# Seven products of quarters for eight in one pair of chunks of a feed-forward layer's first product

## The chip, the cores and the metric

The kernel runs on one core of one Trainium2 chip. The metric is the device time of one execution in microseconds (us). The kernel before was timed in three runs: median 1037.13 us, lowest 1036.57, highest 1037.86.

## The reference, cut to what matters

The reference is a decoder trunk of two layers over 256 tokens of width 1024. Each layer is a half-step feed-forward part, a token mixing and a second half-step feed-forward part, each followed by a layer norm. Only the feed-forward part matters here; it runs four times, and each run is called a stage below.

```python
def swiglu(x, w_in, w_out):
    gate, up = jnp.split(x @ w_in, 2, axis=-1)
    return (jax.nn.silu(gate) * up) @ w_out

x = layer_norm(alpha * x + 0.5 * swiglu(x, ffn_w_in[l, 0], ffn_w_out[l, 0]), ...)
```

Here x is 256 x 1024, w_in 1024 x 5632 and w_out 2816 x 1024, all float32.

## The kernel before

**Arithmetic.** Each float32 operand is split into a high part and a low rest (`split`, L70-81): ScalarE copies the tile to the high part (L78, `wh` or `exh`), VectorE subtracts that from the tile (L79, `wl` or `exl`). A product is then three matmuls on TensorE (`mm3`: L105 high times high, L106 high times low weight, L107 low times high weight). Weights come as tiles of 128x1024 (512 KB), which SyncE's queue loads in the order of its program (`stage`, L82-87) into five buffers `wst`. The split parts live in six buffers `wh`/`wl`, or, for some tiles (`more=True`), in four further buffers `exh`/`exl`.

**First product.** The hidden width is cut into eleven chunks of 256; a chunk is 256 columns of the gate and 256 of the up half, 512 in all. The tokens are two tiles of 128. A chunk takes four weight tiles and 48 matmuls of 128x512: two token tiles, eight steps of 128 along the width 1024, three matmuls each. Chunks 0 and 1 run together, then 2 to 10 one after the other. When a chunk is summed in its PSUM bank, `act` (L248-253) makes silu(gate) on ScalarE (L250) and multiplies by the up half on VectorE (L252). Half-way through the next chunk `emit_T` transposes the result (four matmuls, L270) and splits it (`parts`, L258 on ScalarE, L259 on VectorE); for the chunks in `FAST` it also makes the sums of its quarters that the second product needs (L280-283).

**Second product.** For the chunks in `FAST` (0, 2, 4, 6, 7) `fast(c)` uses seven products of quarters where the plain form has eight: the 256 x 1024 block of weights and the activations are each seen as 2 x 2 quarters, sums of quarters are multiplied, and the seven results are combined at the end (`shared_sums`). The sums of weight quarters go into tiles of their own, `ts` (L353, L354, L357, L358). The other chunks use the plain form (`down`). The last three chunks run as a tail, token tile by token tile, and a layer norm follows.

**What sets the order.** The program is written in the order of the mathematics. A list scheduler orders each engine's instructions before the run; on the chip each engine works through its list in order, and an instruction waits there for its inputs and for the release of the buffer that it writes. PSUM has eight banks: four of `mm`, one each of `pt` and `ov`, two of `sc`.

## Time and profile before

| quantity | value |
|---|---|
| median of three runs | 1037.13 us (1036.57 to 1037.86) |
| the profiled execution: its own time | 1037.3 us |
| its span, first to last instruction | 1035.3 us |
| mean granted TensorE clock in it | 0.997 of full speed |
| TensorE matmul busy | 1018.1 us, 98% |
| VectorE busy | 784.8 us, 76% |
| ScalarE busy | 551.0 us, 53% |
| data read | 188.26 MB, 183 GB/s over the span |

An engine is busy while one of its instructions executes. Matmuls overlap one another, so a busy TensorE is not one at its peak: the distance between the starts of two matmuls tells the rate. Idle time in front of an instruction is shown in square brackets with the instruction that ended it. A stretch of the timeline is named by its time from the start of the span. The fourth stage's first product lies at 843 to 968 us, its second at 968 to 1030.

### The profile page before, as it was taken

The page shows a single profiled execution, that of the slowest core. Times are in us where ns is not written, and L with a number is a line of the kernel's source. Part 1 is how long each engine was busy: PE and PEld are TensorE (multiplying, and loading weights), DVE is VectorE, ACT ScalarE, POOL GpSimd, SP SyncE. Part 2 cuts the span into 40 slices and gives each one's busy share as a digit, 9 for nine tenths or more (in the row PEclk, how much of TensorE's full clock was granted, in tenths as well). Part 3 has the DMA queues.
Part 4 walks back from the last instruction along what each step waited for, and adds up shares of the span by engine and source line. Part 5 has one row for each costly group of instructions (what it writes and reads, how often), then busy time and mean ns, then how long its engine had stood idle before and what let it go on. Part 6 is the DMA issues. An engine that isn't in the chain of part 4 may idle for free.

```text
span 1035.3 us, 14159 instructions
## 1 busy us (share of the span) xinstructions
PE 1018.1 (98%) x5166; PEld 830.0 (80%) x5166; DVE 784.8 (76%) x1313; ACT 551.0 (53%) x916; POOL 23.3 (2%) x35
## 2 busy tenths in 40 slices
PE   9999999999999999999999999999999999999997
PEld 6888878878877888888878888888888778888785
DVE  6765978975989566687986668898679885657877
ACT  7554546435785445553644456544358744446451
POOL 0000000100000000000000000002000000000000
PEclk9999999999999999999999999999999999999998
DMA  9866646753463466674585656559515544666641
GB/s 341 295 204 185 214 148 191 263 189 114 133 230 85 165 189 182 174 232 143 171 283 163 184 183 207 178 156 326 185 34 176 187 136 152 185 190 189 197 150 41
DMA packets 59541, 190.22 MB, mean 184 GB/s; under 512 B 7120, under 2 KB 8784, under 8 KB 58704
## 3 DMA queue, kind: packets, MB, share of 16 engines
q1 hardware_dynamic: 59184, 189.07, 57.8%
q8 instruction: 40, 0.66, 0.3%
q10 hardware_dynamic: 288, 0.26, 0.1%
q14 instruction: 29, 0.24, 0.1%
HBM read 188.26 MB, written 1.05 MB: 183 GB/s over the span
## 4 chain that ended last, share of the span: by engine, by line
PE 73%; DVE 13%; DMA 7%; ACT 4%; issue 2%; DVEq 0%; ACTq 0%; SPq 0%
PE ph L107 12%; PE ph L106 12%; PE ph L105 12%; DMA wst<-in_ffout 5%; DVE wl L79 4%; PE acc L105 4%; PE acc L107 4%; PE acc L106 4%; DVE exl L79 2%; PE pj L107 2%; PE pj L105 2%; PE pj L106 2%; ACT wh L78 2%; PE ov L581 2%; PE pt L569 2%
## 5 line engine op out<-in xcount | busy, mean ns | idle before, releaser
L79 DVE TENSOR_TENSOR wl<-wst,wh 128x1024 fp32r<-128x1024 f32 (+3 forms) x276 | 304.6, 1107 | 147.5 <-ACT wh L78 144.9
L78 ACT ACTIVATE wh<-wst 128x1024 fp32r<-128x1024 f32 (+3 forms) x276 | 264.9, 968 | 233.8 <-PE ph L107 110.8
L105 PE MATMUL ph<-wh,xh 128*128 128x512 f32 x640 | 252.8, 395 | 0.3 <-ACT xh L239 0.3
L107 PE MATMUL ph<-wh,xl 128*128 128x512 f32 x640 | 250.2, 391 | 0.0
L106 PE MATMUL ph<-wl,xh 128*128 128x512 f32 x640 | 250.0, 391 | 0.0
L105 PEld LDWEIGHTS ph<-wh,xh 128*128 128x128 f32 x640 | 120.2, 188 | 25.1 <-ACT wh L154 0.7
L107 PEld LDWEIGHTS ph<-wh,xl 128*128 128x128 f32 x640 | 120.1, 188 | 25.2
L106 PEld LDWEIGHTS ph<-wl,xh 128*128 128x128 f32 x640 | 120.3, 188 | 24.5 <-DVE wl L155 0.3
L78 ACT ACTIVATE exh<-wst 128x512 fp32r<-128x512 f32 (+1 forms) x76 | 63.1, 858 | 65.9 <-PE p L107 54.3
L79 DVE TENSOR_TENSOR exl<-wst,exh 128x512 fp32r<-128x512 f32 (+1 forms) x76 | 72.1, 969 | 28.2 <-ACT exh L78 27.5
L105 PE MATMUL pj<-wh,xh 128*128 128x384 f32 (+3 forms) x224 | 78.2, 349 | 0.3
L107 PE MATMUL pj<-wh,xl 128*128 128x384 f32 (+3 forms) x224 | 77.9, 348 | 0.0
L106 PE MATMUL pj<-wl,xh 128*128 128x384 f32 (+3 forms) x224 | 77.1, 344 | 0.0
L250 ACT ACTIVATE sg<-ph 128x256 f32<-128x256 f32 x88 | 33.5, 384 | 67.1 <-PE ph L107 63.5
L252 DVE TENSOR_TENSOR g<-sg,ph 128x256 f32<-128x256 f32 x88 | 35.3, 416 | 30.0 <-ACT sg L250 29.1
L79 DVE TENSOR_TENSOR exl<-ts,exh 128x1024 fp32r<-128x1024 f32 x40 | 47.5, 1221 | 1.8 <-ACT exh L78 0.5
L105 PEld LDWEIGHTS pj<-wh,xh 128*128 128x128 f32 x224 | 42.3, 189 | 3.1 <-ACT nqS L824 0.7
L106 PEld LDWEIGHTS pj<-wl,xh 128*128 128x128 f32 x224 | 42.4, 189 | 1.8
L107 PEld LDWEIGHTS pj<-wh,xl 128*128 128x128 f32 x224 | 42.3, 189 | 1.8
L78 ACT ACTIVATE exh<-ts 128x1024 fp32r<-128x1024 f32 x40 | 40.7, 1055 | 5.8 <-PE acc L107 3.8
L218 POOL TENSOR_TENSOR mv<-mv,mhalf 128x1 f32<-128x1 f32 x12 | 11.2, 931 | 900.6 <-DVE mv L217 900.6
L548 DVE TENSOR_REDUCE nm<-sc 128x2 f32<-128x512 f32 (+2 forms) x36 | 23.0, 642 | 10.7 <-PE sc L544 10.4
(367 smaller groups left out, 1659.6 us busy)
## 6 DMA issues: line engine op xcount, KB each, us to landing
wst<-in_ffin SPq DMA_DIRECT2D x156, 512.0 KB, 4.4
wst<-in_ffout SPq DMA_DIRECT2D x88, 512.0 KB, 4.0
wst<-in_ffin SPq DMA_DIRECT2D x40, 256.0 KB, 4.0
exh<-in_w SPq DMA_DIRECT2D x16, 512.0 KB, 6.4
wst<-in_w_out SPq DMA_DIRECT2D x16, 512.0 KB, 4.7
gb<-in_lngb SPq DMA_DIRECT2D x6, 1024.0 KB, 7.2
wst<-in_w_b SPq DMA_DIRECT2D x16, 256.0 KB, 4.4
wst<-in_w_nq SPq DMA_DIRECT2D x8, 384.0 KB, 4.4
```

Source lines behind the costliest of these rows:

```text
L78: nc.scalar.activation(h[:, c], src[:, c], AF.Copy)
L79: nc.vector.tensor_tensor(out=l[:, c], in0=src[:, c], in1=h[:, c].bitcast(F32), op=OP.subtract)
L105: nc.tensor.matmul(out, lhsT=xh, rhs=wh, start=start, stop=False)
L106: nc.tensor.matmul(out, lhsT=xh, rhs=wl, start=False, stop=False)
L107: nc.tensor.matmul(out, lhsT=xl, rhs=wh, start=False, stop=stop)
L218: nc.gpsimd.tensor_tensor(out=mv[:, 3:4], in0=mv[:, 2:3], in1=mhalf[:, 0:1], op=OP.pow)
L250: nc.scalar.activation(sg, ps[:, :256], AF.Silu)
L252: nc.vector.tensor_tensor(out=g, in0=sg, in1=ps[:, 256:], op=OP.mult)
L548: nc.vector.tensor_reduce(out=nm[:, :n], in_=sv, axis=AX.X, op=OP.max, negate=True)
L569: nc.tensor.transpose(pt[:, b * P:(b + 1) * P], pr[:, b * P:(b + 1) * P], ident)
L581: order(nc.tensor.matmul(out[g * 64:(g + 1) * 64], lhsT=v, rhs=p_, start=i == 0, stop=i == n - 1, skip_group_check=True))
```

## The change

In each stage chunks 4 and 5 are computed together by `fast_pair`. The weights of the two chunks and the tokens are seen as 2 x 2 quarters: rows of the weights in halves of 512, columns by chunk, tokens by tile. Seven products of quarters replace eight, 84 matmuls of 128x512 for 96. They run in two halves `j`, each over 256 of the 512 rows of a quarter. For each half four weight tiles are loaded (`b00`, `b10`, `b01`, `b11`), four sums of 128x1024 are made in place in those buffers, and seven tiles of 128x1024 are split where four would be. Seven PSUM banks hold the products. At the end ScalarE copies one (`u1`) and VectorE makes seven sums of 128x512 from the banks.

The sums of token quarters are made once a stage after chunks 0 and 1 (`pair_operands`): on VectorE four instructions of 128x1024 and four of 128x512, two of the former being splits, and on ScalarE two copies; they use two of the `wst` buffers for a time, and the split high part has the buffer of the layer norm's gain and bias (`gb`).

`fast(c)` of the second product makes its sums in place in the weight tiles and no longer uses `ts`. Constants and tokens of the first stage are loaded ahead of chunk 3 and not ahead of chunk 4. `g` has four buffers for three, `a10` and `su` one for two.

```diff
+PAIRS = (4,)
...
+            def pair_operands():
...
+                for t in range(2):
+                    r.append(wpool.tile([P, 1024], F32, tag="wst", name="wst", bufs=5))
+                    tt(out=r[t], in0=xTh[t].bitcast(F32).rearrange("p k s -> p (k s)"),
+                       in1=xTl[t].bitcast(F32).rearrange("p k s -> p (k s)"), op=OP.add)
+                tt(out=r[1][:, hi], in0=r[1][:, lo], in1=r[1][:, hi], op=OP.add)
+                tt(out=r[1][:, lo], in0=r[0][:, lo], in1=r[1][:, lo], op=OP.subtract)
+                tt(out=r[0][:, lo], in0=r[1][:, hi], in1=r[0][:, lo], op=OP.subtract)
+                tt(out=r[0][:, hi], in0=r[0][:, hi], in1=r[0][:, lo], op=OP.subtract)
+
+                sh = xpool.tile([P, 2, D], F32R, tag="gb", name="sh")
+                sl = fp.tile([P, 2, D], F32R, tag="sl", name="sl")
+                for t in range(2):
+                    nc.scalar.activation(sh[:, t], r[t], AF.Copy)
+                    nc.vector.tensor_tensor(out=sl[:, t], in0=r[t], in1=sh[:, t].bitcast(F32), op=OP.subtract)
...
+            def fast_pair(c, x, between):
+
+                pr = {}
+                for n in ("p1", "p7", "p2", "p4"):
+                    pr[n] = mm.tile([P, 512], F32, tag="mm", name=n)
+                for n, tag in (("p5", "pt"), ("p6", "ov"), ("p3", "sc")):
+                    pr[n] = at.tile([P, 512], F32, tag=tag, name=n, bufs=2 if tag == "sc" else 1)
+                tt = nc.vector.tensor_tensor
+                for j in range(2):
+                    b00, b10, b01, b11 = (
+                        stage(a["ffin"][l, i, c + h][:, (4 * r + 2 * j) * 512:(4 * r + 2 * j + 2) * 512], 1024)
+                        for h in range(2) for r in range(2))
...
+                    take("p1", b00, True)
+                    tt(out=b00, in0=b01, in1=b00, op=OP.subtract)
+                    tt(out=b01, in0=b11, in1=b01, op=OP.subtract)
+                    take("p5", b00, False)
+                    take("p7", b01, True)
+                    take("p3", b11, False)
+                    tt(out=b11, in0=b11, in1=b00, op=OP.subtract)
+                    take("p6", b11, True)
+                    take("p2", b10, False)
+                    tt(out=b10, in0=b10, in1=b11, op=OP.subtract)
+                    take("p4", b10, True)
+                    for n, y in (("p1", "a00"), ("p5", "s1"), ("p7", "s3"), ("p3", "s4"), ("p6", "s2"), ("p2", "a01"),
+                                 ("p4", "a11")):
+                        for k in range(2):
+                            cols = slice(k * 512, (k + 1) * 512)
+                            mm3(pr[n], (x[y][0][:, 2 * j + k], x[y][1][:, 2 * j + k]), (w[n][0][:, cols], w[n][1][:, cols]),
+                                j == 0 and k == 0, j == 1 and k == 1)
+                    if j == 0:
+                        between()
+                u1, u2, u3, u4 = (fp.tile([P, 512], F32, tag=f"u{n}", name=f"u{n}") for n in range(1, 5))
+                nc.scalar.activation(u1, pr["p1"], AF.Copy)
+                tt(out=u2, in0=u1, in1=pr["p6"], op=OP.add)
...
+                if first and cs[0] == 3:
+                    load_consts()
+                    init_consts()
+                if cs[0] in PAIRS:
+                    pend = fast_pair(cs[0], x_pair, emit_pend)
+                    continue
...
-                if first and cs == (4,):
-                    load_consts()
-                    init_consts()
...
+                if len(cs) == 2:
+                    x_pair = pair_operands()
...
             def fast(c):
...
-                tt(out=u[:, lo], in0=b0[:, hi], in1=b0[:, lo], op=OP.subtract)
-                tt(out=u[:, hi], in0=b1[:, hi], in1=b0[:, hi], op=OP.subtract)
+                tt(out=b0[:, lo], in0=b0[:, hi], in1=b0[:, lo], op=OP.subtract)
+                tt(out=b0[:, hi], in0=b1[:, hi], in1=b0[:, hi], op=OP.subtract)
                 w1 = split(b1, 1024, 1024, True)
-                wu = split(u, 1024, 1024, True)
-                tt(out=v[:, lo], in0=b1[:, hi], in1=u[:, lo], op=OP.subtract)
-                tt(out=v[:, hi], in0=b1[:, lo], in1=v[:, lo], op=OP.subtract)
-                wv = split(v, 1024, 1024, True)
+                wu = split(b0, 1024, 1024, True)
+                tt(out=b1[:, hi], in0=b1[:, hi], in1=b0[:, lo], op=OP.subtract)
+                tt(out=b1[:, lo], in0=b1[:, lo], in1=b1[:, hi], op=OP.subtract)
+                wv = split(b1, 1024, 1024, True)
```

**Where instructions stand.** On VectorE, in the fourth stage, before: the splits of chunk 4's last tile and of chunk 5 (`wl_8673` to `wl_8685` are tiles of chunk 4, `wl_8769` to `wl_8787` those of chunk 5), with the sums and the split of a transposed chunk among them.

```order
L79 TENSOR_TENSOR wl_8685<-wst_8682,wh_8684 128x1024
L259 TENSOR_TENSOR g3l_8629<-ptg_8623,g3h_8628 128x512
L79 TENSOR_TENSOR wl_8769<-wst_8766,wh_8768 128x1024
L252 TENSOR_TENSOR g_8658<-sg_8656,ph_8597 128x256
L252 TENSOR_TENSOR g_8662<-sg_8660,ph_8601 128x256
L79 TENSOR_TENSOR wl_8775<-wst_8772,wh_8774 128x1024
L79 TENSOR_TENSOR wl_8781<-wst_8778,wh_8780 128x1024
L79 TENSOR_TENSOR wl_8787<-wst_8784,wh_8786 128x1024
```

The same place of the changed kernel, the second half of the pair: the four buffers are `wst_8802` (b00), `wst_8804` (b10), `wst_8806` (b01) and `wst_8808` (b11); L81 is the split, L337 to L345 are the sums in place, `wl_8915` and `wl_8921` are the first two tiles of chunk 6.

```order
L337 TENSOR_TENSOR wst_8802<-wst_8806,wst_8802 128x1024
L338 TENSOR_TENSOR wst_8806<-wst_8808,wst_8806 128x1024
L81 TENSOR_TENSOR wl_8817<-wst_8802,wh_8816 128x1024
L81 TENSOR_TENSOR wl_8825<-wst_8808,wh_8824 128x1024
L81 TENSOR_TENSOR exl_8821<-wst_8806,exh_8820 128x1024
L342 TENSOR_TENSOR wst_8808<-wst_8808,wst_8802 128x1024
L261 TENSOR_TENSOR g3l_8799<-ptg_8793,g3h_8798 128x512
L81 TENSOR_TENSOR wl_8834<-wst_8804,wh_8833 128x1024
L81 TENSOR_TENSOR exl_8830<-wst_8808,exh_8829 128x1024
L345 TENSOR_TENSOR wst_8804<-wst_8804,wst_8808 128x1024
L81 TENSOR_TENSOR wl_8915<-wst_8912,wh_8914 128x1024
L81 TENSOR_TENSOR wl_8921<-wst_8918,wh_8920 128x1024
```

Behind these rows stands `exl_8839`, the split for the last product p4 of the pair, so two tiles of chunk 6 and four sums are now ahead of it.

On ScalarE, in the same stage, before: `wh_8485` and `wh_8491` are the high parts of chunk 3's third and fourth tile, `wh_8575` that of chunk 4's first; g0h, s0h and g1h are the parts of chunks 0 and 1.

```order
L78 ACTIVATE wh_8485<-wst_8483 128x1024
L258 ACTIVATE g0h_8364<-ptg_8352 128x384
L258 ACTIVATE s0h_8368<-su_8359 128x512
L78 ACTIVATE wh_8491<-wst_8489 128x1024
L258 ACTIVATE g1h_8435<-ptg_8430 128x512
L78 ACTIVATE wh_8575<-wst_8573 128x1024
```

The same place of the changed kernel: `exh_8719` is the high part of b00 in the first half of the pair, `wh_8616` and `wh_8622` are those of chunk 3's third and fourth tile.

```order
L80 ACTIVATE exh_8719<-wst_8711 128x1024
L260 ACTIVATE g0h_8481<-ptg_8469 128x384
L260 ACTIVATE s0h_8485<-su_8476 128x512
L80 ACTIVATE wh_8616<-wst_8614 128x1024
L80 ACTIVATE wh_8622<-wst_8620 128x1024
L260 ACTIVATE g1h_8566<-ptg_8561 128x512
```

The copy for b00 has moved ahead, and chunk 3's third tile, which was ahead of g0h and s0h, now stands behind both and that copy.

On VectorE in the second product of the fourth stage, before: one chunk of `fast`, its weight tiles being `wst_9511` and `wst_9513`.

```order
L353 TENSOR_TENSOR ts_9515<-wst_9511 128x512
L354 TENSOR_TENSOR ts_9515<-wst_9513,wst_9511 128x512
L357 TENSOR_TENSOR ts_9516<-wst_9513,ts_9515 128x512
L358 TENSOR_TENSOR ts_9516<-wst_9513,ts_9516 128x512
L79 TENSOR_TENSOR wl_9608<-wst_9605,wh_9607 128x1024
L79 TENSOR_TENSOR exl_9518<-wst_9511,exh_9517 128x512
L79 TENSOR_TENSOR exl_9524<-wst_9513,exh_9523 128x1024
```

The same chunk in the changed kernel, with the tiles `wst_9671` and `wst_9673`:

```order
L81 TENSOR_TENSOR exl_9676<-wst_9671,exh_9675 128x512
L438 TENSOR_TENSOR wst_9671<-wst_9671 128x512
L439 TENSOR_TENSOR wst_9671<-wst_9673,wst_9671 128x512
L81 TENSOR_TENSOR exl_9682<-wst_9673,exh_9681 128x1024
L81 TENSOR_TENSOR wl_9764<-wst_9761,wh_9763 128x1024
L81 TENSOR_TENSOR exl_9686<-wst_9671,exh_9685 128x1024
L442 TENSOR_TENSOR wst_9673<-wst_9673,wst_9671 128x512
L443 TENSOR_TENSOR wst_9673<-wst_9673 128x512
L81 TENSOR_TENSOR exl_9692<-wst_9673,exh_9691 128x1024
```

The four sums stood together ahead of the splits; now each stands behind the split that must have read its tile, and both weight buffers stay taken until the last two splits have read them.

## Rows read from the trace of the kernel before

**Rows 1.** The page's first section: busy time, share of the span, instructions.
```profile
PE 1018.1 (98%) x5166; PEld 830.0 (80%) x5166; DVE 784.8 (76%) x1313; ACT 551.0 (53%) x916; POOL 23.3 (2%) x35
```
**Rows 2.** What TensorE waited for: us in total, times, longest.
```profile
PE acc L105 <- DVE g10l L259: 1.8, 3, 1.1
```
**Rows 3.** Timeline of TensorE, fourth stage: start, us, instruction, idle before.
```profile
866.31 0.60 PE L270 MATMUL ptg<-ident,g 128*128 128x128 f32 x4
866.66 0.48 PE L105 MATMUL ph<-wh,xh 128*128 128x512 f32 x1
...
889.31 0.39 PE L107 MATMUL ph<-wh,xl 128*128 128x512 f32 x1
889.54 0.39 PE L105 MATMUL ph<-wh,xh 128*128 128x512 f32 x1
...
912.28 0.39 PE L105 MATMUL ph<-wh,xh 128*128 128x512 f32 x1
...
978.23 0.50 PE L105 MATMUL acc<-wh,g1h 128*128 128x512 f32 x1 [0.44 <-DVE g10l L259]
```
**Rows 4.** Groups by line and shape: busy, mean ns, idle before and releasers.
```profile
L79 DVE TENSOR_TENSOR wl<-wst,wh 128x1024 fp32r<-128x1024 f32 x204 | 249.3, 1223 | 131.8 <-ACT wh L78 129.3
L78 ACT ACTIVATE wh<-wst 128x1024 fp32r<-128x1024 f32 x204 | 215.7, 1060 | 187.4 <-PE ph L107 110.8 <-issue 29.1 <-DMA wst<-in_ffout 28.7
L353 DVE TENSOR_TENSOR ts<-wst 128x512 f32<-128x512 f32 x20 | 13.7, 683 | 0.0
```
**Rows 5.** Timeline of VectorE back to back, fourth stage.
```profile
951.13 0.68 DVE L354 TENSOR_TENSOR ts<-wst 128x512 f32<-128x512 f32 x1
951.73 1.22 DVE L79 TENSOR_TENSOR wl<-wst,wh 128x1024 fp32r<-128x1024 f32 x1
952.87 1.22 DVE L79 TENSOR_TENSOR exl<-wst,exh 128x1024 fp32r<-128x1024 f32 x1
```
**Rows 6.** Timeline of VectorE early in the second, third and fourth stage.
```profile
349.57 0.75 DVE L252 TENSOR_TENSOR g<-sg,ph 128x256 f32<-128x256 f32 x2 [7.77 <-ACT sg L250]
...
532.80 1.23 DVE L79 TENSOR_TENSOR wl<-wst,wh 128x1024 fp32r<-128x1024 f32 x1 [2.61 <-ACT wh L78]
...
861.47 0.75 DVE L252 TENSOR_TENSOR g<-sg,ph 128x256 f32<-128x256 f32 x2 [7.74 <-ACT sg L250]
...
864.92 2.54 DVE L79 TENSOR_TENSOR wl<-wst,wh 128x1024 fp32r<-128x1024 f32 x2
```
**Rows 7.** Busy time by stretch: PE, PEld, DVE, ACT, POOL; clock, DMA share, GB/s.
```profile
863.00:883.00 20.00, 20.00 (x94) 16.53 (x93) 14.31 (x19) 11.49 (x16) 0.00 (x0) 1.00 0.61 192
883.00:903.00 20.00, 20.00 (x94) 16.53 (x93) 12.38 (x19) 10.29 (x15) 0.00 (x0) 1.00 0.65 188
```
**Rows 8.** Timeline of ScalarE ahead of the pair, fourth stage.
```profile
869.71 1.06 ACT L78 ACTIVATE wh<-wst 128x1024 fp32r<-128x1024 f32 x1 [1.70 <-PE ph L107]
870.68 0.47 ACT L258 ACTIVATE g0h<-ptg 128x384 fp32r<-128x384 f32 x1
871.05 0.62 ACT L258 ACTIVATE s0h<-su 128x512 fp32r<-128x512 f32 x1
...
875.69 1.06 ACT L78 ACTIVATE wh<-wst 128x1024 fp32r<-128x1024 f32 x1 [1.71 <-issue]
```
**Rows 9.** The page's DMA issues: KB each, median us to landing.
```profile
wst<-in_ffin SPq DMA_DIRECT2D x156, 512.0 KB, 4.4
```
**Rows 10.** DMA in the stretch 5 to 30 us: packets, MB, mean rate.
```profile
DMA packets 3778, 8.98 MB, mean 359 GB/s; under 512 B 422, under 2 KB 550, under 8 KB 3776
```
**Rows 11.** Chain of work around the fourth stage's second product: start, us, what.
```profile
958.72 4.17 DMA wst<-in_ffout
...
967.73 4.09 DMA wst<-in_ffout
971.85 1.07 ACT wh L78
...
977.57 0.61 DVE g10l L259
```

48 lines of the change are left out of this document (34 added, 14 removed).

## The prediction

> **What bounds the kernel now.** I read the page's busy times first. TensorE is busy 98% of the span and VectorE 76% [rows 1]; a share is no limit yet, so I went on to TensorE's waits. Over all four stages it waits for VectorE in the second product 1.8 us in three waits, and that is its largest entry [rows 2]: TensorE practically never stops. What a matmul costs is read from starts, not from its 0.39 us of duration: 889.31 to 889.54 is one step, and the 96 matmuls and two sets of transposes of two chunks take 912.28 - 889.54 = 22.74 us [rows 3]. With 0.45 us for a set (from 866.31 to 866.66 is 0.35, and the matmul behind it runs 0.09 longer) that is (22.74 - 0.9) / 96 = 0.2275 us a matmul. So an edit that takes matmuls away is worth 0.2275 us each as long as the splits keep ahead.
>
> VectorE is the next engine. In the first product it is busy 14.3 and 12.4 us out of 20 [rows 7], and the split lies well ahead of its use: the high part of chunk 4's first tile is made at 875.69 [rows 8], its first matmul starts at 889.54 [rows 3], 13.85 us later. This lead is what the change draws on. In the second product the chain of waits runs through loads of `wst` (4.17 and 4.09 us), the splits behind them and g10l [rows 11], for which TensorE then waits 0.44 us at 978.23 [rows 3]: there the lead is already nil.
>
> **The change part by part.** *Matmuls.* 12 fewer a stage: 12 x 0.2275 = 2.73 us, 10.9 us in four stages, all on the path as long as TensorE is never made to wait.
>
> *What it adds on VectorE, in the pair.* Six more splits (14 for 8) and eight sums of 128x1024. Back to back a 128x1024 instruction starts 1.14 us behind the one before (951.73, 952.87), a 128x512 one 0.60 (951.13 to 951.73) [rows 5]; 14 x 1.14 = 16.0 us. Then seven sums of 512 from PSUM, 4.2 us by the same step (the nearest row; one that has PSUM as input may cost more). The pair's own demand is 22 x 1.14 = 25.1 us for 84 x 0.2275 + 0.45 = 19.6 us of matmuls; before it was 8 x 1.14 = 9.1 for 22.7. It goes into deficit and lives on the lead. ScalarE gains six copies (1.06 us [rows 4]) and one for u1; it had some 9 us in 20 free [rows 7].
>
> *Which lead is left.* Fourth stage, from the order and the steps above. In the changed list the copy for b00 stands ahead of g0h and s0h, and chunk 3's third tile behind them. b00's load is issued about 866.2, when the first of the splits at 864.92 [rows 6] sets a buffer free, lands 4.4 us later [rows 9] at 870.6, and only then go its copy (1.0 us), g0h and s0h (0.4 and 0.6) and that tile's copy, which started at 869.71 before, ahead of g0h at 870.68 [rows 8]; its split ends at about 875.0. It releases the buffer for b11, the fourth tile of the pair's first half, which lands at 875.0 + 4.4 = 879.4. L338 needs b11, so VectorE stands some 1.4 us before that. From 879.4 it is busy without a pause: nine 1024-instructions left of the first half, thirteen up to and with the split of p4 in the second (two tiles of chunk 6 among them), 22 x 1.14 = 25.1; the transposed chunks' sums and parts and four products by the gate 3.9; waits for copies that ScalarE has just made, 1.3 to 2.3 (each 0.3 to 0.5 us, few). That ends at 909.7 to 910.7.
>
> TensorE comes to p4 of the second half at 889.54 + 42 x 0.2275 + 0.45 + 36 x 0.2275 = 907.7, and needs the low part one matmul later. It stands 1.7 to 2.7 us; I take 2.3, as ScalarE's copy for p4 stands behind that of chunk 6's third tile, whose buffer (b00's) comes free only at about 901.2 and is loaded at 905.6. The first half is not in danger: its p4 split ends near 892.4 and is wanted at 897.7. Behind the pair the u sums and chunk 6's remaining splits cost at most 0.2 us, and by chunk 8 the lead is back, with 7 us of VectorE free in 20.
>
> *Operands of the pair.* 4 x 1.14 + 4 x 0.60 = 7.0 us on VectorE after chunks 0 and 1 start. It fits into an idle stretch of 7.74 us in the fourth stage [rows 6], and of 7.77 in the second [rows 6]. The third shows 2.61 there [rows 6]; 3 to 4 us of splits are pushed back and most of it is made up before chunk 4. I charge 0.2 us: a stall of 2.5 in the third stage, bounds 1.7 to 4.
>
> *First stage.* The constants and tokens (560 and 512 KB) now stand ahead of chunk 2's tiles in SyncE's queue, where DMA already moves 359 GB/s [rows 10]: 1.07 MB / 359 = 3.0 us during which no weights come. Chunk 2 had a lead that just bears this; the pair's b11 is then about 0.7 us later and VectorE starts with less. Stall 3.5 us, bounds 2.7 to 4.5.
>
> *Sums in place in `fast`.* The number of VectorE instructions is the same, but both weight buffers stay taken until the last two splits: for the first about 6 us longer, for the second 1 to 2. In the fourth stage the loads on the chain start when a buffer comes free (958.72, 967.73 [rows 11]), so part of that reaches g10l, which TensorE awaits: 0.4 to 0.75 us a stage, I take 0.5, 2.0 in all. It can be nil if g10l's delay comes from the splits alone, and 1 us if each load of the chain moves.
>
> *At nothing.* `a10`, `su` with one buffer: they are used once in two chunks. The layer norm's gain and bias are loaded when the pair is over, 60 us ahead of their use.
>
> *The sum,* against the profiled execution's 1037.3 us: 1037.3 - 10.9 + (2.3 + 2.3 + 2.5 + 3.5) + 2.0 = 1039.0. The median lies 0.17 us below that execution: 1038.8. With the terms' own ends the forecast runs from 1035.6 to 1042.1.
>
> *A rule beside the step of 1.14 us.* An instruction lasts 1.22 us on VectorE, but the next starts 1.14 behind it [rows 4, 5]. The Trainium skill, "VectorE: DVE Perf Modes", in its section on the DRAIN, says that the next instruction does not start until the pipe has emptied; its errata section gives (N + 151) / 0.96 ns for such an fp32 instruction, 1.224 us for 1024 by my estimate, which is this trace's duration [rows 4] and not its step. By the page's sum 22 instructions would cost 26.9 us, the stall would be 1.8 us longer in each stage and the total 1046, which is rival B. The measured step decides.
>
> **The rivals.** *A, VectorE keeps ahead.* For it: in the first product it is idle a third of the time [rows 7], and 13.85 us of lead stand against a deficit of 25.1 + 3.9 - 19.6 = 9.4; were b11 to land 2 us earlier, nothing would be late. Against it: the lead ends with the load of b11, by the order above. If stalls shrink to between nothing and 1.2 us a stage, the time is 1026.4 (1037.3 - 10.9) to about 1034; middle 1030.
>
> *B, the pair is late (slower).* The split of p4 comes 4 to 5 us after its time. Place: the second half, from b11's landing on; price 4.5 x 4 = 18 us, so 1037.3 - 10.9 + 18 + 2 = 1046.4. It decides once loads take over 6 us instead of 4.4 or the effective step is 1.22: a stall above 2.73 us a stage makes the pair a loss by itself. For it: four of five weight buffers are held by one half. Against: 0.65 of DMA is used in these stretches [rows 7] and 4.4 us is the median landing [rows 9].
>
> *C, buffers of the second product (slower).* Each of the held buffers delays the next load and TensorE stands 1 to 2 us more than now in each stage: 2 to 6 us above the forecast, 1041 to 1045. It decides if the loads at 958 and 967 [rows 11] shift by the full time that the first buffer is held longer.
>
> *D, seven products do not save.* The matmuls of the pair could start further apart, since their token operands come from other tiles; at 0.26 us (0.2275 x 96 / 84) the gain is nil and so are the stalls: 1037.3 + 2.0 = 1039. Against it: 5166 weight loads take 830.0 us [rows 1], 0.16 each, under a step of 0.2275.
>
> **How the numbers follow.** Within 0.2% (2.1 us, about what a measurement of this kernel can tell from no change) means 1035.1 to 1039.2. Forecast 0.44, of it 0.25 within and 0.19 above; A 0.33, all below 1035.1; B 0.10 and C 0.08, above; D 0.05, within. That is faster 0.33, same 0.30, slower 0.37. The range leaves out the lower half of A's span and the upper part of B: 1029 to 1046. The likeliest case's own range is 1035.6 to 1042.1.
>
> **What would show it.** Matmuls in the profile after: 48 fewer. Each step: a wait of TensorE for `exl` (the split for p4 or p6) of 2 to 3 us once in a stage, at the end of the pair; VectorE busy nearly all of the 28 us before it, and idle for a DMA landing (b11) just ahead of that stretch; chunk 6 beginning about 0.4 us earlier than now relative to chunk 4 (22.3 us for 22.74); g10l's wait in the second product at about 1 us for 0.44. If no wait for `exl` is there, A holds; if it is 4 us or more, B; if the waits grow behind 968 us, C; if the step within the pair is above 0.23, D. Wrong altogether would be a scheduler's list that the chip meets in another rhythm: b11 landing by 877, or a stall on a PSUM bank that the pair holds.

## The result and the profile after

The changed kernel takes 1065.43 us (median of 4 runs, 1062.98 to 1071.13) and the kernel before 1037.02 (median of four, one run more than above): a ratio of 1.0281, with a 95% interval of 1.0235 to 1.0326. It is slower by some 28 us. The prediction was 1038.8 with a range of 1029 to 1046, so both the time and the range were wrong. The profiled execution is the one of 1062.98 us, with a span of 1060.9 and a mean granted clock of 0.992 (before: 1035.3 and 0.997).

The page's busy line, which answers [rows 1]:

```profile
PE 1019.8 (96%) x5118; PEld 823.4 (78%) x5118; DVE 888.8 (84%) x1429; ACT 581.8 (55%) x952; POOL 22.3 (2%) x35
```

There are 48 matmuls fewer (5118 for 5166), as the diff says, yet TensorE is busy 1.7 us longer. With less to do it ran part of the time at the lower clock. What it waited for (us in total, times, longest), against [rows 2]:

```profile
PE acc L107 <- DVE g10l L261: 9.2, 4, 3.2
PE pt L240 <- DVE x L229: 9.2, 3, 6.8
PE p L107 <- ACT exh L80: 2.5, 4, 1.0
PE p L108 <- DVE exl L81: 2.4, 6, 0.5
```

L261 is the line that was L259, L229 was L227, and `p` are the banks of the pair's products. g10l, 1.8 us before, is now 9.2. The second row is new in size: the layer norm's output `x`, 6.8 us in one piece (the kernel before waits 0.8 us for it in all). The waits in the pair, around which the prediction was built, come third and fourth.

The same in TensorE's timeline (start, us, instruction, idle before), [rows 3] being its counterpart. The rows of the first block lie in the third stage's second product, the one of the second at the layer norm that ends the first stage:

```profile
669.69 0.51 PE L107 MATMUL acc<-wh,g1h 128*128 128x512 f32 x1 [3.23 <-DVE g10l L261]
...
672.10 0.63 PE L109 MATMUL acc<-wh,g1l 128*128 128x512 f32 x1
672.53 0.63 PE L107 MATMUL acc<-wh,g1h 128*128 128x512 f32 x1
...
```

```profile
201.53 1.97 PE L240 MATMUL pt<-ident,x 128*128 128x128 f32 x8 [6.78 <-DVE x L229]
```

From 672.10 to 672.53 is one step: 0.43 us, where the same step is 0.2275 at the full clock. This wait is paid twice, first as idle time and then at half rate.

To tell the stages' parts apart I use two stretches. "First" runs from TensorE's first transposition of chunk 0's result to that of chunk 10's (107.66 us in each stage before). "Rest" runs from there to the next stage's first transposition, the last one to the end of the span (219.12, 78.21, 218.37 and 61.32 us before); it holds the second product, the layer norm and the attention. Differences to before in us, profiled execution against profiled execution (the medians differ from these by a few us), for the kernels that carry the argument:

| kernel | first, stages 1 to 4 | sum | rest, stages 1 to 4 | sum |
|---|---|---|---|---|
| after | +2.3 −0.7 +1.0 +1.3 | +3.8 | +10.0 +2.8 +7.2 +1.3 | +21.3 |
| `e1_inplace`: sums in place, no pair | 0 0 0 0 | 0 | +8.9 +4.8 +5.7 +5.6 | +24.9 |
| `e2_pair`: pair, sums as before | +2.3 −1.6 −0.9 −2.3 | −2.4 | −1.7 +0.3 +3.8 −0.6 | +1.8 |
| `e9_pair_nosums`: `e2_pair` without its eight sums | −0.8 −2.6 −2.6 −2.6 | −8.6 | −1.7 +0.4 −0.2 −0.1 | −1.7 |
| `e16_three_pairs`: best version | 0 −1.6 +1.2 −2.3 | −2.7 | −1.0 −0.4 −0.2 −0.3 | −2.0 |

The loss of the changed kernel lies almost wholly in "rest", a part of the stage in which not one matmul was removed.

### The profile page after: what moved, and what is told of

Its sections match the earlier page's. It is cut to its first block, busy times and chain, and to the rows that moved or that the text cites. A ratio compares the mean times of both kernels' runs of the same rounds, so it can differ in the third digit from the quotient of the medians.

```text
span 1060.9 us, 14190 instructions
## 1 busy us (share of the span) xinstructions
PE 1019.8 (96%) x5118; PEld 823.4 (78%) x5118; DVE 888.8 (84%) x1429; ACT 581.8 (55%) x952; POOL 22.3 (2%) x35
## 3 DMA queue, kind: packets, MB, share of 16 engines
q1 hardware_dynamic: 59184, 189.07, 54.3%
## 4 chain that ended last, share of the span: by engine, by line
PE 54%; DVE 20%; DMA 13%; issue 7%; ACT 6%; POOL 0%; DVEq 0%; ACTq 0%; SPq 0%; POOLq 0%
DMA wst<-in_ffin 6%; DMA wst<-in_ffout 5%; PE ph L109 5%; PE ph L108 5%; DVE wl L81 5%; PE ph L107 5%; DVE exl L81 4%; PE acc L107 4%; PE acc L109 4%; PE acc L108 4%; PE pj L109 3%; PE pj L107 3%; PE pj L108 3%; ACT wh L80 3%; PE ov L666 2%
## 5 line engine op out<-in xcount | busy, mean ns | idle before, releaser
L81 DVE TENSOR_TENSOR wl<-wst,wh 128x1024 fp32r<-128x1024 f32 (+3 forms) x268 | 290.6, 1100 | 64.4 <-ACT wh L80 63.2
L80 ACT ACTIVATE exh<-wst 128x1024 fp32r<-128x1024 f32 (+1 forms) x148 | 137.5, 954 | 121.3 <-DVE wst L443 36.4
L107 PE MATMUL ph<-wh,xh 128*128 128x512 f32 x512 | 202.1, 397 | 1.9 <-ACT wh L80 1.6
L108 PE MATMUL ph<-wl,xh 128*128 128x512 f32 x512 | 201.1, 393 | 0.6 <-DVE wl L81 0.3
L109 PE MATMUL ph<-wh,xl 128*128 128x512 f32 x512 | 200.9, 392 | 0.0
L81 DVE TENSOR_TENSOR exl<-wst,exh 128x1024 fp32r<-128x1024 f32 (+1 forms) x148 | 158.5, 1089 | 37.4 <-ACT exh L80 36.8
L107 PEld LDWEIGHTS ph<-wh,xh 128*128 128x128 f32 x512 | 96.4, 189 | 22.4 <-ACT wh L80 1.9
L108 PEld LDWEIGHTS ph<-wl,xh 128*128 128x128 f32 x512 | 96.5, 189 | 20.9 <-DVE wl L157 0.8
L109 PEld LDWEIGHTS ph<-wh,xl 128*128 128x128 f32 x512 | 96.4, 188 | 20.1 <-DVE xl L242 0.2
L633 DVE TENSOR_REDUCE nm<-sc 128x2 f32<-128x512 f32 (+2 forms) x36 | 22.9, 642 | 10.4 <-PE sc L629 10.1
L272 PE MATMUL ptg<-ident,g 128*128 128x128 f32 x176 | 27.0, 274 | 1.3 <-DVE g L254 1.3
L272 PEld LDWEIGHTS ptg<-ident,g 128*128 128x128 f32 x176 | 21.8, 141 | 8.2 <-DVE g L254 2.2
```

The costliest lines, as they stand in the source:

```text
L80: nc.scalar.activation(h[:, c], src[:, c], AF.Copy)
L81: nc.vector.tensor_tensor(out=l[:, c], in0=src[:, c], in1=h[:, c].bitcast(F32), op=OP.subtract)
L107: nc.tensor.matmul(out, lhsT=xh, rhs=wh, start=start, stop=False)
L108: nc.tensor.matmul(out, lhsT=xh, rhs=wl, start=False, stop=False)
L109: nc.tensor.matmul(out, lhsT=xl, rhs=wh, start=False, stop=stop)
L272: nc.tensor.transpose(pt[:, at_[k][t]], gs[t][:, k * P:(k + 1) * P], ident)
```

## The experiments

Names in the diffs are those of the kernel after. In the quoted expectations a letter stands for a theory; what each holds is told around them. Each ratio is to the kernel before on the same chip.

**Which part of the change costs the time.** Three theories stood against each other: the sums in place in `fast`, VectorE's deficit in the pair, and the earlier loads of the constants. The first run leaves the pair out and keeps the sums in place. The second keeps the pair and makes the sums in `ts` again, for which `sl` has to share these two buffers. The third loads the constants ahead of chunk 4 as before.

```diff
 e1_inplace (against after)
-PAIRS = (4,)
+PAIRS = ()
...
 e2_pair (against after)
-                sl = fp.tile([P, 2, D], F32R, tag="sl", name="sl")
+                sl = [fp.tile([P, D], F32R, tag="ts", name="sl", bufs=2) for _ in range(2)]
...
-                tt(out=b0[:, lo], in0=b0[:, hi], in1=b0[:, lo], op=OP.subtract)
+                tt(out=u[:, lo], in0=b0[:, hi], in1=b0[:, lo], op=OP.subtract)
 e3_consts4 (against after)
-                if first and cs[0] == 3:
+                if first and cs[0] == 4:
```

> The changed kernel without the pair and its operands; the sums in place of the second product stay, as do the loading of the constants ahead of chunk 3 and the buffer counts. Theory S (the sums in place cost the time: a sum must wait until the split has read the tile it overwrites, and the weight buffers and the memset on GpSimd that waits for a split buffer push the layer norm's hand-over back): the kernel is slower than before by 18 to 25 us, 1055 to 1062, and shows the long wait of TensorE for the layer norm at the end of the first stage and the waits for g10l. Theory V (VectorE's deficit in the pair is never made up and carries into the second product): without the pair the time is that of before, 1036 to 1040.

> The changed kernel with the pair, but the second product's sums in buffers of their own again (two of 128x1024, shared in time with the low parts of the pair's operands). Theory S: the pair by itself costs 2 to 5 us (its measured stalls less the 10.9 us of matmuls saved), so 1038 to 1043, and the waits for g10l and for the layer norm are those of before. Theory V: the time stays near the changed kernel's, 1058 to 1066.

> The changed kernel with the constants and tokens of the first stage loaded ahead of chunk 4 and not ahead of chunk 3. Theory L (that load is what makes the pair of the first stage late, +2.2 us where stage 2 has -0.7): 2 to 3 us less than the changed kernel in the first stage. Rival: the first stage's DMA is full anyway and the load only moves into the pair's own tiles: no gain, or 1 to 3 us more.

`e1_inplace`: 1062.01 us, ratio 1.0230 [1.0209, 1.0252]. `e2_pair`: 1037.23, 1.0002 [0.9988, 1.0016]. `e3_consts4`: 1065.84, 1.0260 [1.0229, 1.0291]. So the sums in place cost 24.5 us by themselves, the pair by itself nothing that can be measured, and where the constants are loaded does not matter in the kernel after. `e1_inplace` still has its constants and its buffer counts, but so has `e2_pair`, where they cost nothing. The waits of `e1_inplace` are nearly those of the kernel after: the row for `x` is the same to the digit, and

```profile
PE acc L107 <- DVE g10l L261: 8.9, 4, 3.0
```

**What the wait for g10l is made of.** The matmul that waits multiplies chunk 1 and does not read g10l. By the program it is the first to write a fourth `acc` bank; `acc` and chunk 10's transposition `ptg` share the four `mm` banks, and g10l is the last to read that transposition. So the wait has two ends: when g10l is done, and how early TensorE's list brings that matmul.

First VectorE's end. The kernel before, its timeline in the fourth stage: the first and the last of the four sums of the second product's chunk 2 (L353 to L358), the last split ahead of which it stands idle, and g10l.

```profile
959.87 0.68 DVE L353 TENSOR_TENSOR ts<-wst 128x512 f32<-128x512 f32 x1
...
965.20 0.69 DVE L358 TENSOR_TENSOR ts<-wst,ts 128x512 f32<-128x512 f32 x1
...
972.94 1.23 DVE L79 TENSOR_TENSOR wl<-wst,wh 128x1024 fp32r<-128x1024 f32 x1 [1.55 <-ACT wh L78]
...
977.49 0.68 DVE L259 TENSOR_TENSOR g10l<-ptg,g10h 128x512 fp32r<-128x512 f32 x1
```

The sums only read the weight tiles, so they run as soon as these have landed, and are over 11.6 us before g10l. In `e1_inplace` three of the same four sums (L438, L439, L442) stand here; the fourth, L443, follows behind g10l:

```profile
993.97 1.23 DVE L81 TENSOR_TENSOR wl<-wst,wh 128x1024 fp32r<-128x1024 f32 x1 [3.69 <-ACT wh L80]
995.11 0.68 DVE L81 TENSOR_TENSOR exl<-wst,exh 128x512 fp32r<-128x512 f32 x1
995.83 0.69 DVE L438 TENSOR_TENSOR wst<-wst 128x512 f32<-128x512 f32 x1
996.44 1.22 DVE L81 TENSOR_TENSOR exl<-wst,exh 128x1024 fp32r<-128x1024 f32 x1
997.57 0.69 DVE L439 TENSOR_TENSOR wst<-wst 128x512 f32<-128x512 f32 x1
998.29 0.69 DVE L442 TENSOR_TENSOR wst<-wst 128x512 f32<-128x512 f32 x1
998.90 0.68 DVE L261 TENSOR_TENSOR g10l<-ptg,g10h 128x512 fp32r<-128x512 f32 x1
```

L438 overwrites a half tile that the split in the row above it (995.11, to 995.79) reads; it starts at 995.83. So a sum in place cannot run before the tile's own split, and the split waits for ScalarE's copy. VectorE is idle for 3.69 us ahead of these rows, and what ends this idle time is a load of a weight tile, for which the copy waits:

```profile
992.87 1.06 ACT L80 ACTIVATE wh<-wst 128x1024 fp32r<-128x1024 f32 x1 [3.05 <-DMA wst<-in_ffout]
```

From the split behind that copy (993.97) to g10l are 4.93 us, with three sums and two splits between. In the kernel before (972.94 to 977.49) they are 4.55 us, with three splits between. Both numbers are the same in all four stages, so the sums right ahead of g10l cost 0.4 us a stage.

Now TensorE's end, in the kernel before and then in `e1_inplace`; the row that waits for g10l before, at 978.23, is in [rows 3]:

```profile
973.97 0.60 PE L270 MATMUL ptg<-ident,g 128*128 128x128 f32 x4
...
977.40 0.39 PE L106 MATMUL acc<-wl,g1h 128*128 128x512 f32 x1
```

```profile
994.00 0.60 PE L272 MATMUL ptg<-ident,g 128*128 128x128 f32 x4
...
996.29 0.40 PE L109 MATMUL acc<-wh,g1l 128*128 128x512 f32 x1
999.64 0.79 PE L107 MATMUL acc<-wh,g1h 128*128 128x512 f32 x1 [2.96 <-DVE g10l L261]
```

Before, 14 matmuls stand between the transposition and the matmul that waits, and TensorE comes to it 3.8 us behind the transposition. In `e1_inplace` and in the kernel after they are nine, and TensorE comes to it after 2.7 us, in every stage. The waits for g10l grow by 7.1 us in `e1_inplace`. By this count 4.5 of them (four times 1.14 us) come from the changed order of TensorE's list, 1.5 from the sums ahead of g10l, and the rest, about 1, from loads that land later. The lists are made before the run, so the sums in place act here through the scheduler's order; no run changed TensorE's order alone.

ScalarE's side in the kernel after, fourth stage:

```profile
1009.02 1.06 ACT L80 ACTIVATE exh<-wst 128x1024 fp32r<-128x1024 f32 x1 [1.43 <-PE p L109]
...
1013.92 1.06 ACT L80 ACTIVATE exh<-wst 128x1024 fp32r<-128x1024 f32 x1 [2.52 <-DVE wst L443]
```

The copies wait by turns for a product (a split buffer comes free) and for a sum in place (L443). The wait for a product was there before (54.3 us over the kernel, now 33.3). The second is new in size; the kernel after, and then the largest of its kind in the kernel before:

```profile
ACT exh L80 <- DVE wst L443: 36.4, 20, 3.1
```

```profile
ACT exh L78 <- DVE ts L354: 1.3, 3, 0.5
```

What the wait of 2.96 us then cost, in `e1_inplace` (stretch, us, busy of PE, PEld, DVE, ACT, POOL; granted clock, DMA share, GB/s):

```profile
997.00:999.60 2.60, 0.00 (x0) 0.00 (x0) 2.56 (x5) 1.31 (x2) 0.00 (x0) 0.85 0.40 156
999.60:1002.00 2.40, 2.36 (x6) 1.88 (x7) 2.40 (x3) 1.28 (x2) 0.00 (x0) 0.50 0.23 29
1002.00:1004.00 2.00, 2.00 (x6) 1.59 (x5) 1.68 (x2) 0.47 (x1) 0.00 (x0) 0.50 0.74 246
1004.00:1006.00 2.00, 2.00 (x7) 1.54 (x6) 0.00 (x0) 0.00 (x0) 0.00 (x0) 0.59 0.88 291
1006.00:1008.00 2.00, 2.00 (x10) 1.66 (x9) 0.43 (x1) 0.63 (x1) 0.00 (x0) 1.00 0.55 209
```

TensorE idles, and the granted clock is 0.50 until past 1004: six matmuls in 2 us where ten go later. Over the whole kernel the clock's mean is 0.987 over 1060.9 us for 0.997 over 1035.3; that is 13.8 − 3.1 = 10.7 us of full clock lost, my estimate from the means. The two waits above are 18.1 us, for 2.6 before (1.8 and 0.8); 15.5 and 10.7 make 26.2, where the spans differ by 25.6. The price of a wait in clock is not fixed: in the profiled execution of the kernel after the same two waits (18.4 us) went with a clock of 0.992, some 5.4 us lost by the same sum.

**Whose buffers: three ways to give the sums room.** Two theories: the weight tiles are held too long and loads come late, or the sums in place wait for splits that wait for split buffers. `e5_wv_own` keeps the sums in place but gives the last split buffers of its own; `e6_weights7` loads the first weight tile into buffers of its own (two more weight buffers in effect); `e7_u_inplace` and `e8_v_inplace` put half of the sums back into `ts`, the v ones and the u ones.

```diff
 e5_wv_own (against e1_inplace)
-                wv = split(b1, 1024, 1024, True)
+                wv = tuple(fp.tile([P, 1024], F32R, tag="ts", name="wv" + q, bufs=2) for q in "hl")
...
 e6_weights7 (against e1_inplace)
+                b0 = fp.tile([P, 1024], F32, tag="ts", name="ts", bufs=2)
+                nc.sync.dma_start(out=b0, in_=src[:, 2 * c * 1024:(2 * c + 1) * 1024])
 e7_u_inplace (against e1_inplace)
-                tt(out=b1[:, hi], in0=b1[:, hi], in1=b0[:, lo], op=OP.subtract)
+                tt(out=v[:, hi], in0=b1[:, hi], in1=b0[:, lo], op=OP.subtract)
...
 e8_v_inplace (against e1_inplace)
-                tt(out=b0[:, lo], in0=b0[:, hi], in1=b0[:, lo], op=OP.subtract)
+                tt(out=u[:, lo], in0=b0[:, hi], in1=b0[:, lo], op=OP.subtract)
...
```

> Sums in place without the pair (the first experiment), and the high and low part of v, the last split of a fast chunk, go to two buffers of their own in the memory that the sums had before, not to the four shared split buffers. Theory B (a sum in place must wait for the split that reads the tile it overwrites, and that split waits for one of four split buffers, which only a finished product of TensorE sets free: the sums, done early in idle time before, now stand right ahead of g10l): with the fifth pair of buffers the time comes back most of the way, 1037 to 1044. Theory W (the weight buffers, taken longer, are what is short): no change against the first experiment, 1057 to 1064.

> Sums in place without the pair, and the first weight tile of each fast chunk is loaded into two further buffers of 128x1024, in the memory that the sums had before: seven weight buffers for five in the second product. Theory W: the time comes back, 1037 to 1044. Theory B: it stays near the first experiment's 1062, within 1054 to 1064.

> Without the pair; of the four sums of a fast chunk only the first two (u) are made in place in the first weight tile, v goes to buffers of its own. Theory B: u waits only for the first split of a half tile and v not at all for the second's, so most of the loss goes: 1037 to 1045. Theory W: the first tile is the one held about 6 us longer, so most of the loss stays: 1052 to 1064.

> Without the pair; only the last two sums (v) are made in place in the second weight tile, u goes to buffers of its own. Theory B: v must wait for the split of the whole second tile, so most of the loss stays: 1050 to 1063, with the layer norm's idle stretch at the end of the first stage. Theory W: the second tile is held only 1 to 2 us longer, so little is lost: 1037 to 1045.

`e5_wv_own`: 1042.16 us, ratio 1.0045 [1.0029, 1.0062]; its runs spread from 1037.76 to 1046.40 and the profiled one is the fastest, with "first" and "rest" each within 0.1 of before in sum; where the others lose their 5 us it cannot show. `e6_weights7`: 1047.58, 1.0103 [1.0084, 1.0121]. `e7_u_inplace`: 1048.14, 1.0107 [1.0091, 1.0123]. `e8_v_inplace`: 1054.26, 1.0168 [1.0148, 1.0188]. Split buffers for the last split give back 19 to 20 of the 24.5 us, which speaks for the chain of split buffers; but two weight buffers give back 13 to 14, more than that theory allowed. `e6_weights7` and `e7_u_inplace` lie in neither theory's range. Each of the two means breaks the same ring (buffer, copy, split, sum, next copy) at another place, and either theory alone was too narrow. What they change is that g10l is done sooner, in `e6_weights7` 2.4 us behind the transposition where it took 3.9 to 4.9 before; in `e5_wv_own` TensorE's list still has nine matmuls there. The v sums alone in place cost 17 and the u ones alone 11, which is more than both together, so the two parts do not add. Of the 11 us 4.4 lie in "first", where TensorE waits for `g` ahead of a transposition once in each stage (3.8 us in all), and the clock is 0.998: its waits for g10l, four of up to 1.7 us, cost no clock.

The wait lists of `e6_weights7` hold no row for g10l at all. Its second long wait stays, 9.2 us for `x` in three with 6.8 the longest, just as it is after (and `e8_v_inplace` has 9.1 us of it).

So there is a second cause behind "rest", and it is not g10l.

**The layer norm.** GpSimd's timeline at the end of the first stage, before and then after:

```profile
185.29 0.92 POOL L218 TENSOR_TENSOR mv<-mv,mhalf 128x1 f32<-128x1 f32 x1 [184.46 <-DVE mv L217]
187.46 0.96 POOL L479 MEMSET exl<- 128x1024 f32 x1 [1.24 <-PE acc L106]
```

```profile
192.53 0.96 POOL L564 MEMSET exl<- 128x1024 f32 x1 [191.70 <-PE acc L108]
193.52 0.56 POOL L220 TENSOR_TENSOR mv<-mv,mhalf 128x1 f32<-128x1 f32 x1
```

Before, the layer norm's power (L218) comes first and the memset behind it. After, the memset, which clears a split buffer for the attention and waits until TensorE has done with it, stands ahead of the power (L220) in GpSimd's list. On the chip the power comes only some 1.4 us late by this: its input is ready at 192.10 and it runs at 193.52. The larger part is VectorE's list, which was laid out for that order: token tile 0's last step (L229) stands behind the second tile's L223, and so starts at 200.73, 6.65 us behind the end of the power.

```profile
197.77 1.40 DVE L223 SCALAR_TENSOR_TENSOR x<-x,mv,gb 128x512 f32<-128x512 f32 x2
200.73 2.73 DVE L229 SCALAR_TENSOR_TENSOR x<-x,mv,gb 128x512 f32<-128x512 f32 x4
```

TensorE has nothing to transpose until 201.53, and then runs at the low clock (columns as above, kernel after):

```profile
195.00:200.00 5.00, 0.00 (x0) 0.00 (x0) 5.00 (x11) 0.00 (x0) 2.07 (x6) 1.00 0.96 330
200.00:205.00 5.00, 3.47 (x15) 2.96 (x15) 5.00 (x9) 1.20 (x2) 0.10 (x1) 0.51 1.02 366
205.00:210.00 5.00, 5.00 (x25) 4.67 (x24) 2.24 (x4) 1.20 (x2) 0.00 (x0) 0.81 1.03 387
```

Moving this one memset to VectorE takes it out of GpSimd's list. I did so in the kernel after, in `e6_weights7`, and in the kernel after together with `e6_weights7`'s buffers; a last run makes chunk 7's v outside the weight tile as well.

```diff
 e4_memset (against after), e12_w7_memset (against e6_weights7)
-                nc.gpsimd.memset(z, 0.0)
+                (nc.vector if z is E else nc.gpsimd).memset(z, 0.0)
 e10_pair_w7_memset (against after)
-                sl = fp.tile([P, 2, D], F32R, tag="sl", name="sl")
+                sl = [fp.tile([P, D], F32R, tag="ts", name="sl", bufs=2) for _ in range(2)]
...
+                b0 = fp.tile([P, 1024], F32, tag="ts", name="ts", bufs=2)
...
+                (nc.vector if z is E else nc.gpsimd).memset(z, 0.0)
 e13_v7_out (against e12_w7_memset)
+                v = fp.tile([P, 1024], F32, tag="v7", name="v7") if c == FAST[-1] else b1
```

> The changed kernel with one memset per layer moved from GpSimd to VectorE: that of the buffer E of the token mixing, 128x1024, which takes a split buffer that a product of the second product must first release. Theory S, its second half (the power of the layer norm stands behind this memset on GpSimd, so the first token tile's layer norm ends only behind the second's and TensorE has nothing to do): 8 to 12 us less than the changed kernel, 1052 to 1057, with the idle stretch of 6.8 us at the end of the first stage gone; the waits for g10l stay. Rival: the layer norm is late because VectorE is, and the time stays within 2 us of the changed kernel's.

> The whole change (pair and sums in place), with two edits: the first weight tile of a fast chunk is loaded into two further buffers (shared in time with the low parts of the pair's operands), and the memset of E is on VectorE. Theory S in two halves (weight buffers for g10l, the list of GpSimd for the layer norm): both waits go and the pair's own saving is left: 1030 to 1038. Rival (the two losses are one, a late VectorE, and what is taken away at one place comes back at the next): above 1045.

> The sums in place without the pair, with the two further weight buffers and the memset of E on VectorE. Theory S in two halves: nothing of the loss of 24.5 us is left, 1034 to 1040. Rival (the layer norm's loss is VectorE's, not the list's): it stays at the 1047.6 of the run with the two buffers alone, 1045 to 1049.

> The last run of sums in place (two more weight buffers, the memset of E on VectorE), with one edit: for the last fast chunk, 7, v goes to a buffer of its own. Theory T (the 6 us still lost there lie at the layer norms, because v of chunk 7 waits for the split of its second tile, so the last two products, their sums and the layer norm come some 2 us later in each stage): 1036 to 1040. Rival (those 6 us come from the sums in place of all chunks): within 1.5 us of 1043.3.

`e4_memset`: 1060.60 us, 1.0218 [1.0194, 1.0242], 4.8 us less than after, and less than expected (8 to 12): the wait of 6.78 is gone (the longest for `x` is 1.3), but g10l's rises to 10.1. The two kernels' intervals overlap slightly; `e12_w7_memset` settles it. `e12_w7_memset`: 1043.32, 1.0059 [1.0044, 1.0074]: 4.3 of the 10.5 us of `e6_weights7` come back, between what the two theories allowed. `e13_v7_out`: 1040.48, 1.0032 [1.0022, 1.0043]: with chunk 7's v out of the weight tile some 2.5 us more come back, all in "rest", which fits the theory that its sum and split in place delay the end of the second product and with it the layer norm (it lies half a us above that theory's range). The rest, about 3.5 us at the layer norms of the first and third stage, I could not place. `e10_pair_w7_memset`: 1043.73, 1.0065 [1.0050, 1.0080]: of the 28 us of the kernel after 22 are undone by two buffers and one memset; the pair's own saving, which the theory expected on top, is not seen.

**The pair by itself.** Two theories on `e2_pair`'s even result: seven products save their 2.73 us a stage and VectorE takes it back, or they save nothing. `e9_pair_nosums` leaves out the eight sums of quarters, so that the raw quarters are multiplied; its time is that of 84 matmuls with a lighter VectorE. `e11_pair5` puts the pair one chunk later.

```diff
 e9_pair_nosums (against e2_pair)
-                    tt(out=b00, in0=b01, in1=b00, op=OP.subtract)
-                    tt(out=b01, in0=b11, in1=b01, op=OP.subtract)
...
 e11_pair5 (against e2_pair)
-PAIRS = (4,)
+PAIRS = (5,)
```

> The pair with the second product's sums in buffers of their own (the second experiment), and the eight sums of weights that each stage's pair makes on VectorE are left out, so the pair multiplies the raw quarters; its splits, loads and products stay. Theory P (VectorE's demand in the pair is what takes the gain of the pair away): with 8 x 1.14 = 9.1 us less on VectorE a stage TensorE no longer waits in the pair, and of 10.9 us saved most is seen: 1027 to 1031. Rival D (the products themselves save nothing, or the loads bound the pair): within 2 us of the second experiment's 1037.

> The second experiment with chunks 5 and 6 as the pair and not 4 and 5. Theory P: VectorE has one chunk more (11.4 us of matmuls, of which it needs about 7) to build up its lead ahead of the pair, above all in the first stage, where the pair lost 2.3 us: 1033 to 1036. Rival: the lead is bounded by the buffers, not by time, so the place does not matter: 1036 to 1039.

`e9_pair_nosums`: 1028.47 us, 0.9916 [0.9900, 0.9933]; "first" is 2.6 us shorter in stages 2 to 4, where 2.73 was forecast. The saving is real and the eight sums take it back; whether by VectorE's time or by the order that they add to the loads and splits, this run does not part. `e11_pair5`: 1044.86, 1.0075 [1.0060, 1.0090], which neither theory expected. Its first products gain 5.1 us, twice those of `e2_pair`, but the time comes back in the second product, where the copy ahead of g10l waits 2.6 to 3.8 us for a weight load in each stage, for 0.8 to 1.9 in the kernel before. That it is the pair's deficit that delays these loads is likely and not shown.

```profile
PE acc L107 <- DVE g10l L261: 9.7, 4, 3.0
```

**Towards a better version.** `e14_pair_w6` takes `e2_pair` and gives `fast` a sixth weight buffer in the memory of `u3` and `u4`; `e15_pair_w6_gps` moves one of the pair's sums to GpSimd; `e16_three_pairs` leaves the pair out in the first stage, where it loses, and loads the constants ahead of chunk 4 again.

```diff
 e14_pair_w6 (against e2_pair)
+                u34 = fp.tile([P, 1024], F32, tag="u34", name="u34")
+                u3, u4 = u34[:, :512], u34[:, 512:]
...
+                b0 = fp.tile([P, 1024], F32, tag="u34", name="b0")
 e15_pair_w6_gps (against e14_pair_w6)
-                    tt(out=b01, in0=b11, in1=b01, op=OP.subtract)
+                    nc.gpsimd.tensor_tensor(out=b01, in0=b11, in1=b01, op=OP.subtract)
 e16_three_pairs (against e14_pair_w6)
+            pairs = () if first else PAIRS
...
-                if first and cs[0] == 3:
+                if first and cs[0] == 4:
```

> The pair with the second product's sums in buffers of their own (the second experiment), and the first weight tile of a fast chunk is loaded into a sixth buffer, in the memory that two of the pair's own sums (u3, u4) leave free by then. Theory W2 (a weight buffer more brings g10l forward, as the run with seven showed, whether the sums are in place or not): the waits for g10l, 2.8 us and the low clock behind one of them in the second experiment, go: 1031 to 1035. Rival: the one buffer is taken in turn by the chunks and nothing comes forward: 1036 to 1039.

> The same, and of each half's four sums of weights one (b11 less b01, for p7) is made on GpSimd, 2 of 8 a stage. Theory P (the pair is bound by VectorE's demand): 2.3 us less on VectorE a stage, 1 to 2 us of the pair's stall gone in each: 1027 to 1033. Rival (GpSimd is slow enough that p7's split waits for it, or it slows VectorE): 1035 or more.

> The pair with six weight buffers (the run before last), but in the first stage chunks 4 and 5 are computed as before, without the pair and its operands, and the constants are loaded ahead of chunk 4 again. In that run's trace the first stage's pair is a loss of 3.7 us, those of the other stages -2.4, +0.5 and -2.5. Theory L (in the first stage, where the DMA is full, VectorE never has the lead that a pair uses up): 1030 to 1033. Rival (the loss there is the start-up's and only shows at the pair): 1034 to 1037.

`e14_pair_w6`: 1035.30 us, 0.9982 [0.9973, 0.9992]; g10l's wait falls to 0.3 us, and "rest" is 1.6 us shorter than before. It lies just above its expected range. `e15_pair_w6_gps`: 1042.42, 1.0046 [1.0034, 1.0059]: the sum takes 2.40 us on GpSimd, and the split behind it comes late.

```profile
L339 POOL TENSOR_TENSOR wst<-wst 128x1024 f32<-128x1024 f32 x8 | 19.2, 2399 | 197.3 <-DVE wst L338 117.6 <-DMA wst<-in_ffin 79.6
```

`e16_three_pairs`: 1033.27 (1031.43 to 1034.83), 0.9956 [0.9939, 0.9973]. It is faster than both kernels, than the one before by some 3.7 us: three pairs keep 2.7 of their 8.2 us, "rest" is 2.0 us shorter with the sixth buffer, and no wait for g10l is left. It lies between its two theories' ranges, a little nearer to the first.

## Why the prediction was wrong, point by point

**The step that failed** is the term "sums in place in `fast`", charged with 0.5 us a stage and 2.0 in all, with bounds of nil and 4 us. It measured 24.5 us alone. The prediction noted that the number of VectorE instructions is the same, and it is (1313 in `e1_inplace`, as in [rows 1]); it asked how much longer the weight buffers are held, and for how long g10l would shift by that. It never asked when a sum may now run, and what the scheduler would then make of the lists. Four things were missed:

- Writing in place adds an order: sum behind split, split behind copy, and the next copy behind the sum. `e5_wv_own` and `e6_weights7` bear it out: with buffers of their own for the last split, or with two more for the weights, the sums may stay in place and 19 and 14 of the 24.5 us come back.
- With that order the lists of other engines changed. TensorE comes to the matmul that needs g10l's bank 1.1 us sooner in each stage, which makes 4.5 of the 7.1 us by which the waits for g10l grew. This is counted from the traces; no run put TensorE's list back alone.
- A wait can cost more than its length, since the clock is 0.50 behind some of them: in `e1_inplace` 15.5 us of added waits came with some 10.7 us of lost clock, in the kernel after 15.8 with some 5.4. The sum charged stalls at their length.
- The layer norm behind the second product. The memset was not in the diff and nothing in the prediction spoke of GpSimd's list, though the changed order of GpSimd's and VectorE's lists could be read from the program's lists; it cost 6.78 us of idle time and some 5 us at the lower clock; `e4_memset` and `e12_w7_memset` gave back 4.8 and 4.3 us.

**Rival C** had the right place, the second product, and the right sign. Its price (1 to 2 us a stage) came from the delay of two loads, and gave 1041 to 1045. A row that could have warned is in the prediction itself: "there the lead is already nil" for g10l [rows 3, 11]. Where the lead is nil, a new order has no cover and its bound is not the length of one load. Its mechanism, loads that come late, was at work as well: the copy ahead of g10l waits 1.6 to 3.3 us for a weight load in the kernel after, 0.8 to 1.9 before.

**The likeliest case's own range,** 1035.6 to 1042.1, is not what the terms' ends add up to: they give some 1034 to 1044. The measured time lies outside either.

**The matmuls were right.** 2.73 us a stage was forecast, and 2.6 is what `e9_pair_nosums` shows. Rival D, that seven products save nothing, falls; the step within the pair stays at 0.23 (`e2_pair`, start, us):

```profile
910.13 0.39 PE L109 MATMUL p<-wh,xl 128*128 128x512 f32 x1
910.35 0.39 PE L107 MATMUL p<-exh,xh 128*128 128x512 f32 x1
910.66 0.50 PE L108 MATMUL p<-exl,xh 128*128 128x512 f32 x1
```

**The pair's stalls were right in kind, and in the fourth stage in place.** Stall means here 2.73 plus the change of "first". In the kernel after it is 5.0, 2.0, 3.7 and 4.0 us in stages 1 to 4, 14.7 in all, where 3.5, 2.3, 2.5 and 2.3 were forecast, 10.6 in all; in `e2_pair` 5.1, 1.1, 1.8 and 0.5, 8.5 in all. The first stage is the worst, as said, and worse than said.

In the kernel after the fourth stage goes as the prediction counted it. VectorE waits for b11 ahead of the stretch, and TensorE for p4 at its end:

```profile
902.62 1.23 DVE L338 TENSOR_TENSOR wst<-wst 128x1024 f32<-128x1024 f32 x1 [0.99 <-DMA wst<-in_ffin]
...
932.18 1.23 DVE L81 TENSOR_TENSOR exl<-wst,exh 128x1024 fp32r<-128x1024 f32 x1 [0.50 <-ACT exh L80]
```

```profile
932.20 0.49 PE L107 MATMUL p<-exh,xh 128*128 128x512 f32 x1 [1.00 <-ACT exh L80]
...
933.46 0.50 PE L108 MATMUL p<-exl,xh 128*128 128x512 f32 x1 [0.53 <-DVE exl L81]
```

The fourth stage's transpositions stand 23.07 us later than in the kernel before (889.38 for 866.31). So L338 starts at 879.55 in the times of the kernel before, where b11 was to land at 879.4. From there to the end of p4's split are 30.79 us, where the sum had 30.3 to 31.3 (909.7 to 910.7 less 879.4). The count of instructions at 1.14 us was sound: by the sum of the rule on the DRAIN that the prediction weighed the stretch would have been 1.8 us longer. The section that holds this rule in the Trainium skill, "VectorE: DVE Perf Modes", section "The DRAIN you can't avoid", itself adds that a next instruction which is not held starts earlier; the prediction left that out, and with it the Trainium skill has room for the step of 1.14 us. TensorE's two waits are 1.5 us for the 2.3 forecast. What the sum lacked is the low clock behind them (a granted clock of 0.50 and 0.66 over 2 us each, last section), some 1.7 us by my estimate from these two; with it 3.2 of the 4.0 us are placed.

In `e2_pair` the same place costs nothing. Its low part is ready just in time, and TensorE loses 0.1 us (0.31 between 910.35 and 910.66 above, for 0.23). VectorE's own rows there:

```profile
879.56 1.23 DVE L339 TENSOR_TENSOR wst<-wst 128x1024 f32<-128x1024 f32 x1
...
909.38 1.23 DVE L81 TENSOR_TENSOR exl<-wst,exh 128x1024 fp32r<-128x1024 f32 x1 [0.20 <-ACT exh L80]
```

L339, which needs b11, starts at 879.56 without idle time ahead of it. The transpositions stand 2.44 us later than before (868.75 for 866.31), so this is 877.1 in the times of the kernel before, some 2.4 us earlier than in the kernel after. From there to the end of p4's split are 31.05 us.

Why b11 comes so much later beside sums in place, and why the other stages' pairs stall more there ("first" +3.8 us for −2.4 in sum), was not settled. The two parts measured alone make 24.1 us, and together they cost 28.4.

**The operands and the first stage.** For the operands 0.2 us was charged, a stall of 2.5 us in the third stage for 2.3 in the fourth. It measured 3.7 for 4.0 in the kernel after and 1.8 for 0.5 in `e2_pair`, so these runs do not tell what the operands cost. The constants ahead of chunk 3 were blamed for the first stage: `e3_consts4` shows no gain from putting them back, so in the kernel after that step was not the cause. In `e16_three_pairs` constants and pair were taken out together, and what either is worth there is open.

## What to carry to other kernels

A sum that writes into its input is not free because the number of instructions is the same: write down what it must now wait for, and follow that wait to the buffers that set it free, before pricing how long a buffer is held. The order of lists shows such a move before any run; compare it on every engine of a hand-over, GpSimd's too, and not only where the diff has lines. On TensorE count the matmuls between a hand-over's start and the instruction that needs its result or its buffer: five fewer made the larger part of a wait here. A term whose place has no lead left gets a wide bound on the slow side, and a stall of TensorE may cost more than its length: 1.3 and 1.7 times in the two kernels above, no more than its length in `e7_u_inplace`.
